# A two-layer hybrid encoder on one core: the start of layer 1 in written order up to the keys' product

## The chip, the core and the metric

One core of a Trainium2 chip runs the whole kernel: TensorE (PE) multiplies, VectorE (DVE), ScalarE (ACT) and GpSimd (POOL) work on tiles, SyncE (SP) issues most loads. The metric is the device time of one execution in microseconds (us), as the median of several runs. Before the change it is 1549.28 us, the median of 3 runs from 1547.82 to 1549.66.

## The reference, cut to what matters

Two layers are applied to 512 tokens of width 1024, all in float32. Each layer has a mixer (a Mamba-2 state-space part in both directions and windowed attention with 16 heads and 4 key-value heads) and a gated FFN. The piece that this case is about is the first stage of a layer:

```python
h = rms_norm(x, norm1_w[i])
proj = h @ w_in[i]
z, xbc, dt_raw, q, k, v = jnp.split(proj, [...], axis=-1)
xbc = jax.nn.silu(depthwise_conv_centered(xbc, conv_w[i], conv_b[i]))
dt = jax.nn.softplus(dt_raw + dt_bias[i])
a = -jnp.exp(a_log[i])
y_fwd = ssd_chunked(xs, dt[:, :, 0], a[0], bm, cm)
```

`ssd_chunked` needs running sums of `dt * a` over the tokens of a chunk of 128.

## The kernel before, in words

**Tiles.** The 512 tokens are four tiles of 128. A product in float32 is made of three float32r matmuls (`mm3`, lines 278 to 280 before): high part by high part, high by low, low by high. So each weight unit (a `raw` tile of at most 128 x 1024, one or two loads on SP's queue) is split by ScalarE into a high part (`whi`, line 161) and by VectorE into the rest (`wlo`, line 162), and each activation likewise.

**Weight units.** `prep_raw` issues the loads and `prep_split` the splits, in the order of a list: three units "vdt" (values and dt columns, 3, 3 and 2 of the 8 slices of the contraction), two "k" (keys), two each of bc0, q0, xa0 and so on. Three `raw` buffers and three pairs of split buffers are used in turn, so k0's split takes the buffers of vdt unit 0, and k0's load the `raw` buffer that vdt unit 0's split has freed.

**The first stage of layer 1.** `first_norm(t)` squares a token tile (ScalarE), makes the inverse root (POOL), scales the tile (VectorE), transposes it on TensorE and splits it (`turn_split`, lines 314 to 318) into `hT`. `vdt(t, j)` multiplies token tile t by unit j: 9, 9 or 6 matmuls of 288 columns. `bias_table` makes the table of the attention's bias. After the 96 matmuls of vdt, `setup` transposes the convolution's parameters with 42 small transposes (line 271), `dt_step` is softplus (one activation on ScalarE and 18 small operations on VectorE, lines 546 to 558), `dt_sums` makes the running sums by six matmuls with triangles of ones (line 574), `dt_own` takes logarithms (lines 593 to 601), and the keys, bc0, q0 and xa0 are each 48 matmuls of 512 columns, 24 by each of their two units (`ws_part`). `k_done` copies the keys out (lines 620 and 622).

**What sets the order.** In layer 1 the instructions up to the end of vdt stand under `tc.manual_schedule()`: each engine takes them in the order of the code. From there on (`start.close()`) a scheduler orders them by priority. Every engine works through its queue in order. A load on a hardware queue waits for the one issued eight loads before it.

Of the kernel before, what the change touches and what calls it, by code (L numbers as in the profile page):

```python
# [7 lines left out]
F32 = mybir.dt.float32  # L8
# [6 lines left out]
P = 128  # L15
L = 512
NT = L // P
D = 1024
# [21 lines left out]
WBUF = 3  # L40
RBUF = 3
# [5 lines left out]
def encoder_kernel(  # L47
# [23 lines left out]
    nc = tc.nc  # L71
# [21 lines left out]
    def nm(s):  # L93
        uid[0] += 1
        return f"{s}_{uid[0]}"
# [12 lines left out]
    splits = {}  # L108
# [26 lines left out]
    def prep_raw(n):  # L135
        while pos["raw"] < min(n, len(units)):
            key, (w, pieces) = units[pos["raw"]]
            raw = rawp.tile([P, 1024], F32, tag="raw", name=nm("raw"))
            for kt0, nkt, c0, ncol, off, pitch in pieces:
                dst = raw[:, : nkt * pitch].rearrange("p (k c) -> p k c", k=nkt)  # L140
                nc.sync.dma_start(dst[:, :, off : off + ncol], kcols(w, kt0, nkt, c0, ncol))
            raws[key] = raw
            pos["raw"] += 1
# [93 lines left out]
    wrow = npool0.tile([1, D], F32, name="wrow")  # L237
    nc.scalar.dma_start(wrow, norm1_w[0:1])
    nc.sync.dma_start(x_sb[0], x_in[0:P])
    prep_raw(1)  # L240
    nc.sync.dma_start(x_sb[1], x_in[P : 2 * P])
    prep_raw(2)
    nc.sync.dma_start(x_sb[2], x_in[2 * P : 3 * P])
    prep_raw(3)
    nc.sync.dma_start(x_sb[3], x_in[3 * P : 4 * P])

    ones = cp.tile([P, P], F32, name="ones")
    G.memset(ones, 1.0)
# [40 lines left out]
        G.tensor_tensor(rs, ms, mhalf.broadcast_to([P, width]), ALU.pow)  # L289
        return rs  # L290

    def first_norm(t):

        xn = npool0.tile([P, D], F32, tag="xn", name=nm("xn"), bufs=2)
        ss = smp.tile([P, 1], F32, tag="ss1", name=nm("ss"))
        S.activation(xn, x_sb[t], AF.Square, scale=1.0 / 32.0, accum_out=ss)
        rs = smp.tile([P, 1], F32, tag="rs1", name=nm("rs"))
        G.tensor_scalar(rs, ss, EPS, None, ALU.add)
        G.tensor_tensor(rs, rs, mhalf, ALU.pow)
        yield  # L300
        for b in range(2):
            cs = slice(512 * b, 512 * b + 512)
            V.scalar_tensor_tensor(xn[:, cs], x_sb[t][:, cs], rs, wb0[:, cs], ALU.mult, ALU.mult)
        yield
        for b in range(2):
            turn_split(xn, t, b, hT)
        yield

    def turn_split(xn, t, b, dst):
        ps = small_bank()  # L310
        pv = ps.rearrange("p (k c) -> p k c", k=4)
        for j in range(4):
            kt = 4 * b + j
            turn128(pv[:, j, :], xn[:, kt * P : (kt + 1) * P], ident)
        h, l = dst[b]
        hs, ls = h[:, :, t * P : (t + 1) * P], l[:, :, t * P : (t + 1) * P]
        S.copy(hs, pv)
        V.tensor_tensor(ls, pv, f(hs), ALU.subtract)
# [105 lines left out]

    def bcast(name, src, width):
        t = cp.tile([P, width], F32, name=name)
        nc.scalar.dma_start(t, src.unsqueeze(0).broadcast_to([P, width]))
        return t

    dtb_all = bcast("dtb_all", dt_bias.rearrange("a b c -> (a b c)"), DEPTH * 32)  # L430
# [39 lines left out]
    for i in range(DEPTH):  # L470
        side = Side()
        with ExitStack() as mix:
            ep = mix.enter_context(pool(f"mixer_{i}", bufs=1, reuse_waits="tile"))

            def g_ws(key, acts, done):

                banks = [dense_bank() for _ in range(2)]
                for j in range(2):
                    ws_part(key, j, acts, banks)
                    if j == 1:  # L480
                        done(banks)
                    yield
# [11 lines left out]
            def vdt(t, j):  # L494
                k0, n = ((0, 3), (3, 3), (6, 2))[j]
                hv, lv = (w[:, : n * 288].rearrange("p (k c) -> p k c", k=n) for w in vw[j])
                sl = slice(t * P, (t + 1) * P)
                for k in range(n):
                    kt = k0 + k
                    ah, al = hT[kt // 4]  # L500
                    mm3(vb[t][:, :288], ah[:, kt % 4, sl], al[:, kt % 4, sl], hv[:, k], lv[:, k], kt == 0, kt == KT - 1)
                if j == 2:
                    S.copy(v_sb[:, t, :], vb[t][:, :256])
                    V.tensor_tensor(xdt[:, t, :], vb[t][:, 256:288], dtb_all[:, 32 * i : 32 * i + 32], ALU.add)

            if i == 0:
                norms = [first_norm(t) for t in range(NT)]
                next(norms[0])
                next(norms[0])
                prep_split(1)  # L510
                next(norms[0])
                next(norms[1])
                next(norms[1])
                prep_split(2)
                next(norms[1])
                next(norms[2])
                next(norms[2])
                prep_split(3)
                vw = [splits.pop((i, "vdt", j)) for j in range(3)]
                vdt(0, 0)  # L520
                vdt(1, 0)
                vdt(0, 1)
                next(norms[2])
                next(norms[3])
                next(norms[3])
                vdt(1, 1)
                vdt(0, 2)
                vdt(1, 2)
                prep_raw(WBUF + RBUF)
                bias_table()  # L530
                next(norms[3])
                for t in (2, 3):
                    for j in range(3):
                        vdt(t, j)
                S.activation(expa_all, alog_all, AF.Exp)
                start.close()
            else:
                vw = [take((i, "vdt", j)) for j in range(3)]
                for t, j in ((t, j) for t in range(NT) for j in range(3)):
                    vdt(t, j)  # L540
# [3 lines left out]
            def dt_step():  # L544

                V.scalar_tensor_tensor(sp_e, xdt, -1.0, xdt, ALU.mult, ALU.min)
                S.activation(sp_e, sp_e, AF.Exp)
                V.tensor_scalar(sp_w, sp_e, 2.0, None, ALU.add)
                V.reciprocal(sp_w, sp_w)
                V.tensor_tensor(sp_w, sp_w, sp_e, ALU.mult)  # L550
                V.tensor_tensor(sp_w2, sp_w, sp_w, ALU.mult)
                V.tensor_scalar(sp_a, sp_w2, 1.0 / 17.0, None, ALU.mult)
                for n in (15, 13, 11, 9, 7, 5, 3):
                    V.scalar_tensor_tensor(sp_a, sp_a, 1.0 / n, sp_w2, ALU.add, ALU.mult)
                V.scalar_tensor_tensor(sp_a, sp_a, 1.0, sp_w, ALU.add, ALU.mult)
# [47 lines left out]
            if i == 0:  # L603
                setup()
                setupx.close()
                first.close()
            dt_step()


            mixA = []  # L610
# [10 lines left out]
                    for o in (0, HD):  # L621
                        V.tensor_tensor(kst_l[o : o + HD, h], src, f(kst_h[r : r + HD, h]), ALU.subtract)

            side.run(g_ws((i, "k"), hT, k_done), 0)

            class Item:
                pass
# [526 lines left out]
```

## Time and profile before

| | us |
|---|---|
| median of 3 runs | 1549.28 |
| lowest and highest run | 1547.82, 1549.66 |
| the profiled execution's own time | 1550.88 |
| its span | 1549.2 |
| mean granted clock of TensorE | 0.992 of full |

The profiled execution took 1.60 us more than the median, and 1.68 of its time lie around the span. In the rows below, times run from the span's start. A row of a timeline has the start and length in us, engine, line, operation, output<-inputs, partitions x elements, and in brackets the rest before it and what ended it. A row of a stretch has from:to, its length, the busy time of each engine with its instructions, and at the end the granted TensorE clock as a share of 2.4 GHz, the DMA engines' busy share and GB/s. PEld is the load of weights into TensorE, SPq an issue on SP's queue.

### The profile page before, as it was taken

The numbers are of one execution on the slowest core, as the hardware profiler recorded it, in microseconds if no ns is written. First come the engines' busy times: TensorE is split into PE (matmuls) and PEld (weight loads), VectorE is DVE, ScalarE is ACT, GpSimd is POOL, SyncE is SP. The second block draws the span as 40 slices with busy tenths as digits, with TensorE's granted clock in tenths as the row PEclk, the third lists the DMA queues.
The fourth block names the chain that finished last, engine by engine and source line by source line (L and its number), as shares of the span: only waits on it lengthen the run. The fifth ranks groups of instructions, "written<-read, shape, count | busy, mean of one in ns | idle before, by whom it ended". The sixth has DMA issues, their size and how long they took to land.

```text
span 1549.2 us, 20198 instructions
## 1 busy us (share of the span) xinstructions
PE 1512.3 (98%) x7680; PEld 1241.2 (80%) x7680; DVE 873.1 (56%) x1406; ACT 795.0 (51%) x1464; POOL 176.6 (11%) x246
## 2 busy tenths in 40 slices
PE   7999999999999999999999999999999999999997
PEld 6787778877888888888888777888778888888886
DVE  5677777676644444433367777777666434443333
ACT  4468988873443233323256788788535323332223
POOL 3000002424200000000020000053232000000002
PEclk9899999999999999999999999999999999999999
DMA  6522333453233333333343322345422333333321
GB/s 203 157 82 77 84 85 96 129 181 95 92 100 96 96 99 101 98 98 96 99 148 90 88 77 63 83 123 177 136 96 82 95 97 100 102 96 96 95 95 68
DMA packets 113079, 161.48 MB, mean 104 GB/s; under 512 B 7931, under 2 KB 90107, under 8 KB 112974
## 3 DMA queue, kind: packets, MB, share of 16 engines
q1 hardware_dynamic: 104756, 132.60, 28.0%
q0 software_dynamic: 7648, 27.50, 6.5%
q8 instruction: 60, 0.98, 0.3%
q14 instruction: 37, 0.30, 0.1%
q10 hardware_dynamic: 578, 0.10, 0.0%
HBM read 155.82 MB, written 8.55 MB: 106 GB/s over the span
## 4 chain that ended last, share of the span: by engine, by line
PE 88%; DVE 4%; issue 2%; ACT 2%; POOL 1%; DMA 1%; POOLq 0%; SPq 0%; DVEq 0%; ACTq 0%
PE pd L280 22%; PE pd L278 22%; PE pd L279 22%; PE psm L280 3%; PE psm L278 3%; PE psm L279 3%; PE psm L686 2%; PE psm L676 2%; PE psm L918 1%; PE psm L642 1%; PE psm L933 1%; PE psm L643 1%; PE psm L876 1%; DVE wlo L162 1%; ACT whi L161 1%
## 5 line engine op out<-in xcount | busy, mean ns | idle before, releaser
L278 PE MATMUL pd<-t,whi 128*128 128x512 f32 (+1 forms) x1088 | 420.0, 387 | 1.5 <-ACT whi L161 1.5
L279 PE MATMUL pd<-t,whi 128*128 128x512 f32 (+1 forms) x1088 | 419.4, 386 | 0.0
L280 PE MATMUL pd<-t,wlo 128*128 128x512 f32 (+1 forms) x1088 | 418.7, 385 | 0.4 <-DVE wlo L162 0.4
L162 DVE TENSOR_TENSOR wlo<-raw,whi 128x1024 fp32r<-128x1024 f32 (+1 forms) x214 | 260.5, 1221 | 239.7 <-ACT whi L161 239.0
L161 ACT CAST whi<-raw 128x1024 fp32r<-128x1024 f32 (+1 forms) x214 | 222.1, 1042 | 235.8 <-PE pd L279 207.3
L278 PEld LDWEIGHTS pd<-t,whi 128*128 128x128 f32 x1088 | 205.0, 189 | 40.2 <-ACT whi L161 1.7
L280 PEld LDWEIGHTS pd<-t,wlo 128*128 128x128 f32 x1088 | 204.9, 188 | 39.9 <-DVE wlo L162 1.2
L279 PEld LDWEIGHTS pd<-t,whi 128*128 128x128 f32 x1088 | 205.2, 189 | 37.8 <-issue 0.8
L278 PE MATMUL pd<-whi,t 128*128 128x256 f32 (+2 forms) x544 | 191.2, 351 | 0.0
L279 PE MATMUL pd<-wlo,t 128*128 128x256 f32 (+2 forms) x544 | 181.6, 334 | 4.0 <-DVE wlo L162 3.9
L280 PE MATMUL pd<-whi,t 128*128 128x256 f32 (+2 forms) x544 | 182.2, 335 | 0.6 <-DVE t L958 0.6
L279 PEld LDWEIGHTS pd<-wlo,t 128*128 128x128 f32 x544 | 105.4, 194 | 17.0 <-DVE wlo L162 4.6
L278 PEld LDWEIGHTS pd<-whi,t 128*128 128x128 f32 x544 | 105.3, 194 | 14.5 <-issue 4.6
L280 PEld LDWEIGHTS pd<-whi,t 128*128 128x128 f32 x544 | 105.2, 193 | 11.0 <-DVE t L958 1.5
L1096 ACT CAST ph<-t 128x512 fp32r<-128x512 f32 x40 | 25.0, 624 | 142.9 <-PE psm L279 132.5
L1097 DVE TENSOR_TENSOR pl<-t,ph 128x512 fp32r<-128x512 f32 x40 | 27.7, 692 | 114.8 <-ACT ph L1096 114.8
L395 DVE SCALAR_TENSOR_TENSOR sg<-pd,fprm,sg 128x511 f32<-128x511 f32 x88 | 65.9, 748 | 30.7 <-ACT sg L389 29.0
L644 DVE CUSTOM_DVE_ANT_0 s<-psm,bias,sink_all 128x256 f32<-128x256 f32 (+1 forms) x128 | 66.8, 547 | 24.6 <-POOL s L638 11.3
L658 ACT ACTIVATE s<-s,nm 128x257 f32<-128x257 f32 (+1 forms) x128 | 70.6, 556 | 3.4 <-DVE nm L655 3.2
L395 DVE SCALAR_TENSOR_TENSOR xT<-pd,cprm,xT 128x509 f32<-128x509 f32 (+2 forms) x96 | 67.5, 743 | 3.3 <-ACT xT L389 3.2
L278 PE MATMUL pd<-whi,ph 128*128 128x512 f32 x176 | 68.9, 391 | 0.0
L279 PE MATMUL pd<-wlo,ph 128*128 128x512 f32 x176 | 68.7, 390 | 0.0
(206 smaller groups left out, 2183.2 us busy)
## 6 DMA issues: line engine op xcount, KB each, us to landing
raw<-in_w_up_dram SPq DMA_DIRECT2D x88, 512.0 KB
raw<-in_w_in_dram SPq DMA_DIRECT2D x52, 512.0 KB
raw<-in_w_down_dram SPq DMA_DIRECT2D x44, 512.0 KB
rows<-sums POOLq DMA_DIRECT2D x32, 512.0 KB, 5.7
raw<-in_w_out_dram SPq DMA_DIRECT2D x32, 512.0 KB
bias<-toep POOLq DMA_DIRECT2D x16, 384.0 KB, 3.9
raw<-in_w_in_dram SPq DMA_DIRECT2D x18, 256.0 KB
x<-in_x_dram SPq DMA_DIRECT2D x8, 512.0 KB
```

The costliest lines, as they stand in the source:

```text
L161: S.copy(hi[:, :used], raw[:, :used])
L162: V.tensor_tensor(lo[:, :used], raw[:, :used], f(hi[:, :used]), ALU.subtract)
L278: mm(o, lh, rh, start=start, stop=False)
L279: mm(o, lh, rl, start=False, stop=False)
L280: mm(o, ll, rh, start=False, stop=stop)
L395: V.scalar_tensor_tensor(dst[:, lo:hi], src[:, lo + d : hi + d], taps[k], dst[:, lo:hi], ALU.mult, ALU.add)
L644: V.tensor_tensor_reduce(out=s4[:, h, :w], in0=ps[:, :w], in1=it.bias[h // 2][:, h % 2, it.j0 : it.j1], scale=1.0, scalar=sink4[:, h : h + 1],
L658: S.activation(s4[:, h, : w + 1], s4[:, h, : w + 1], AF.Exp, bias=nm4[:, h : h + 1], accum_out=den[:, h : h + 1])
L676: turn128(ps[:, c : c + P], it.s4[:, h, b * P : (b + 1) * P], ident)
L686: mm(po[c * HD : (c + 1) * HD, :256], v_sb[:, it.k0 // P + b, it.g * HD : (it.g + 1) * HD], it.pts[b][:, c * 256 : (c + 1) * 256], start=( ...
L1096: S.copy(h, p_sb[kt])
L1097: V.tensor_tensor(l, p_sb[kt], f(h), ALU.subtract)
```

## The change

It writes out the order of layer 1's first stage up to and including the keys' product.

- **Loads.** Tokens 0 and 1 are loaded first, then vdt unit 0, token 2, unit 1, token 3, unit 2. The four broadcast loads (dt bias, a_log, skip, sink) go to SP's queue, behind unit 2, instead of ScalarE's.
- **First norms.** The generator `first_norm` becomes `first_square`, `first_scale`, `first_turn`; tile t+1 is squared ahead of tile t's turn, with three buffers `xn` instead of two.
- **Products.** vdt(0,0) stands between the turns of tiles 0 and 1; the others are interleaved anew, by unit for tiles 2 and 3.
- **Keys.** The two keys' units are split as soon as vdt units 0 and 1 are used up, and the manual order goes on through `setup`, the keys' product and `dt_step`; the rest, `dt_sums` included, is left to the scheduler.

```diff
-    prep_raw(1)
-    nc.sync.dma_start(x_sb[1], x_in[P : 2 * P])
...
+    for t in range(1, NT):
+        nc.sync.dma_start(x_sb[t], x_in[t * P : (t + 1) * P])
+        prep_raw(t)
...
-        nc.scalar.dma_start(t, src.unsqueeze(0).broadcast_to([P, width]))
+        nc.sync.dma_start(t, src.unsqueeze(0).broadcast_to([P, width]))
...
             if i == 0:
-                norms = [first_norm(t) for t in range(NT)]
...
+                first_square(0)
+                first_scale(0)
+                first_square(1)
                 prep_split(1)
+                first_turn(0)
+                first_scale(1)
+                vw = [splits.pop((i, "vdt", 0))]
+                vdt(0, 0)
+                first_square(2)
                 prep_split(2)
+                first_turn(1)
+                vw.append(splits.pop((i, "vdt", 1)))
+                vdt(0, 1)
+                vdt(1, 0)
+                vdt(1, 1)
+                first_scale(2)
+                first_square(3)
                 prep_split(3)
+                prep_raw(WBUF + RBUF)
+                vw.append(splits.pop((i, "vdt", 2)))
+                first_turn(2)
+                first_scale(3)
                 vdt(0, 2)
                 vdt(1, 2)
                 bias_table()
+                vdt(2, 0)
+                first_turn(3)
+                vdt(3, 0)
+                prep_split(4)
+                vdt(2, 1)
+                vdt(3, 1)
+                prep_split(5)
+                vdt(2, 2)
+                vdt(3, 2)
                 S.activation(expa_all, alog_all, AF.Exp)
-                start.close()
...
-            dt_step()
+            else:
+                dt_step()
...
-            side.run(g_ws((i, "k"), hT, k_done), 0)
+            keys = g_ws((i, "k"), hT, k_done)
+            if i == 0:
+                next(keys)
+                dt_step()
+                for _ in keys:
+                    pass
+                start.close()
+            else:
+                side.run(keys, 0)
```

**On TensorE, behind vdt, before.** frow and nrow are the last parameter transposes, psm_732 takes the running sums, pd_483 and pd_484 the keys.

```order
L271 MATMUL psm_424<-ident,frow 128x8 x22
L271 MATMUL psm_448<-ident,nrow 128x2 x8
L574 MATMUL psm_732<-sp_406,t_le 128x64
L574 MATMUL psm_732<-sp_406,t_gt 128x64
L574 MATMUL psm_732<-sp_406,t_ge 128x64
L574 MATMUL psm_732<-sp_406,t_lt 128x64
L574 MATMUL psm_732<-sp_406,ones 128x64 x2
L278 MATMUL pd_483<-t_10_121,whi_485 128x512
L279 MATMUL pd_483<-t_11_122,whi_485 128x512
```

The keys' first products stand behind the running sums. The same place now:

```order
L268 MATMUL psm_431<-ident,frow 128x8 x22
L268 MATMUL psm_455<-ident,nrow 128x2 x8
L275 MATMUL pd_472<-t_10_121,whi_370 128x512
L276 MATMUL pd_472<-t_11_122,whi_370 128x512
L277 MATMUL pd_472<-t_10_121,wlo_371 128x512
```

The keys follow the parameter transposes at once. And behind q0 (pd_653 is its second bank, pd_744 the first bank of xa0):

```order
L277 MATMUL pd_653<-t_12_123,wlo_605 128x512
L581 MATMUL psm_732<-sp_413,t_le 128x64
L581 MATMUL psm_732<-sp_413,t_gt 128x64
L581 MATMUL psm_732<-sp_413,t_ge 128x64
L581 MATMUL psm_732<-sp_413,t_lt 128x64
L581 MATMUL psm_732<-sp_413,ones 128x64 x2
L275 MATMUL pd_744<-t_10_121,whi_654 128x512
```

The running sums have moved behind the 144 matmuls of the keys, bc0 and q0.

**On ScalarE, before, from the last copy of the values (v) to the keys' splits.** whi_485 and whi_489 are k0 and k1, whi_493 and whi_526 bc0, the rows named sp are softplus and dt_own, ex is the running sums' exponential.

```order
L503 COPY v_177<-pd_187 128x256
L535 ACTIVATE expa_all<-alog_all 128x64
L547 ACTIVATE sp_406<-sp_406 128x128
L594 ACT_TABLE_LOAD
L594 ACTIVATE sp_409<-sp_407 128x128
L595 ACT_TABLE_LOAD
L595 ACTIVATE sp_408<-sp_409 128x128
L575 ACTIVATE ex_180<-psm_732 128x384
L161 CAST whi_485<-raw_326 128x1024
L577 COPY run_182<-psm_732 128x4x16 x2
L161 CAST whi_489<-raw_328 128x1024
```

Both keys' splits stand behind five activations and two table loads. The same place now, with whi_370 and whi_392 for k0 and k1, whi_474 and whi_525 for bc0 (t_12 is the last token tile's split):

```order
L319 CAST t_12_123<-psm_354 128x4x128
L161 CAST whi_370<-raw_294 128x1024
L161 CAST whi_392<-raw_296 128x1024
L505 COPY v_177<-pd_186 128x256
L505 COPY v_177<-pd_187 128x256
L543 ACTIVATE expa_all<-alog_all 128x64
L161 CAST whi_474<-raw_298 128x1024
L554 ACTIVATE sp_413<-sp_413 128x128
L161 CAST whi_525<-raw_478 128x1024
```

The keys' splits stand in front of the last copies of the values and of softplus; dt_own's two table loads stand further down.

**On SP, the first loads before.** x_1 to x_4 are the token tiles, raw_94, raw_98 and raw_102 the vdt units (two loads each), crow the first of nine parameter loads.

```order
L239 DMA x_1_87<-in_x_dram 128x1024
L141 DMA raw_94<-in_w_in_dram 128x3x256
L141 DMA raw_94<-in_w_in_dram 128x3x32
L241 DMA x_2_88<-in_x_dram 128x1024
L141 DMA raw_98<-in_w_in_dram 128x3x256
L141 DMA raw_98<-in_w_in_dram 128x3x32
L243 DMA x_3_89<-in_x_dram 128x1024
L141 DMA raw_102<-in_w_in_dram 128x2x256
L141 DMA raw_102<-in_w_in_dram 128x2x32
L245 DMA x_4_90<-in_x_dram 128x1024
L457 DMA crow<-in_conv_w_dram 7x1536
```

Tokens and units alternate from the first on. Now, with raw_95, raw_99 and raw_103 for the units:

```order
L239 DMA x_1_87<-in_x_dram 128x1024
L241 DMA x_2_88<-in_x_dram 128x1024
L141 DMA raw_95<-in_w_in_dram 128x3x256
L141 DMA raw_95<-in_w_in_dram 128x3x32
L241 DMA x_3_89<-in_x_dram 128x1024
L141 DMA raw_99<-in_w_in_dram 128x3x256
L141 DMA raw_99<-in_w_in_dram 128x3x32
L241 DMA x_4_90<-in_x_dram 128x1024
L141 DMA raw_103<-in_w_in_dram 128x2x256
L141 DMA raw_103<-in_w_in_dram 128x2x32
L429 DMA dtb_all<-in_dt_bias_dram 128x64
L429 DMA alog_all<-in_a_log_dram 128x64
```

Tile 1 stands in front of unit 0, and the four broadcasts (two more follow) in front of the parameters. Behind the first attention blocks of layer 1 every engine has the order it had before.

## Rows read from the trace of the kernel before

**Rows 1.** The page: busy time of the engines, us, share of the span, instructions.
```profile
PE 1512.3 (98%) x7680; PEld 1241.2 (80%) x7680; DVE 873.1 (56%) x1406; ACT 795.0 (51%) x1464; POOL 176.6 (11%) x246
```

**Rows 2.** Stretches, from:to and length, then busy time and instructions of each engine.
```profile
15.05:35.57 20.52, 20.52 (x158) 19.11 (x156) 9.66 (x21) 8.22 (x18) 5.16 (x9) 1.00 0.51 161
35.57:40.46 4.89, 0.01 (x1) 0.03 (x1) 4.44 (x15) 0.62 (x1) 2.02 (x5) 0.57 1.02 323
40.46:44.77 4.31, 2.80 (x13) 2.61 (x13) 1.30 (x7) 3.38 (x7) 0.00 (x0) 0.50 1.00 289
44.77:50.69 5.92, 5.92 (x15) 4.68 (x16) 3.81 (x5) 2.06 (x4) 0.00 (x0) 0.57 0.79 246
```

**Rows 3.** Timeline of TensorE: start, length, line, tiles, count, rest before it.
```profile
34.94 0.63 PE L271 MATMUL psm<-ident,nrow 2*128 2x2 f32 x8
40.46 0.66 PE L574 MATMUL psm<-sp,t_le 128*128 128x64 f32 x2 [4.89 <-DVE sp L593]
...
79.96 0.39 PE L278 MATMUL pd<-t,whi 128*128 128x512 f32 x1
```

**Rows 4.** Waits from 33 to 50 us: in total, times, longest.
```profile
PE psm L574 <- DVE sp L593: 4.9, 1, 4.9
```

**Rows 5.** Timelines of VectorE and ScalarE: softplus begins, k0's split.
```profile
34.26 0.29 DVE L546 SCALAR_TENSOR_TENSOR sp<-xdt 128x128 f32<-128x128 f32 x1
...
44.74 1.23 DVE L162 TENSOR_TENSOR wlo<-raw,whi 128x1024 fp32r<-128x1024 f32 x1 [0.57 <-ACT whi L161]
...
43.68 1.04 ACT L161 CAST whi<-raw 128x1024 fp32r<-128x1024 f32 x1
```

**Rows 6.** Layer 2: running sums and next product on TensorE, and a stretch.
```profile
835.41 0.33 PE L574 MATMUL psm<-sp,t_le 128*128 128x64 f32 x2
...
836.66 0.48 PE L278 MATMUL pd<-t,whi 128*128 128x512 f32 x1
...
800.00:850.00 50.00, 49.53 (x240) 41.45 (x239) 37.91 (x72) 30.95 (x48) 0.00 (x0) 1.00 0.38 106
```

**Rows 7.** The start: timelines of TensorE, ScalarE and VectorE.
```profile
13.43 1.97 PE L314 MATMUL psm<-ident,xn 128*128 128x128 f32 x8 [3.83 <-DVE xn L303]
...
18.80 0.44 PE L278 MATMUL pd<-whi,t 128*128 128x288 f32 x1
19.04 0.37 PE L279 MATMUL pd<-wlo,t 128*128 128x288 f32 x1
...
19.51 0.29 PE L279 MATMUL pd<-wlo,t 128*128 128x288 f32 x1
19.64 0.29 PE L280 MATMUL pd<-whi,t 128*128 128x288 f32 x1
...
25.29 1.23 PE L314 MATMUL psm<-ident,xn 128*128 128x128 f32 x8
...
4.43 1.06 ACT L296 ACTIVATE xn<-x 128x1024 f32<-128x1024 f32 x1 [1.58 <-DMA x<-in_x_dram]
...
8.68 0.91 ACT L161 CAST whi<-raw 128x864 fp32r<-128x864 f32 x1 [3.10 <-DMA raw<-in_w_in_dram]
...
26.60 0.69 DVE L318 TENSOR_TENSOR t<-psm,t 128x512 fp32r<-128x512 f32 x1 [0.34 <-ACT t L317]
```

**Rows 8.** Two stretches of rest; the granted clock is the third number from the end.
```profile
36.25:36.50 0.25, 0.00 (x0) 0.00 (x0) 0.21 (x1) 0.00 (x0) 0.25 (x1) 0.51 1.05 311
287.05:288.75 1.70, 0.00 (x0) 0.00 (x0) 1.43 (x2) 1.68 (x2) 0.23 (x1) 1.00 0.00 0
```

**Rows 9.** Timeline of SP's queue: loads issued.
```profile
0.80 0.39 SPq L239 DMA_DIRECT2D x<-in_x_dram  x1
...
2.24 0.49 SPq L241 DMA_DIRECT2D x<-in_x_dram  x1
...
10.84 0.37 SPq L457 DMA_DIRECT2D crow<-in_conv_w_dram  x1
...
16.96 38.48 SPq L141 DMA_DIRECT2D raw<-in_w_in_dram  x9
```

More of the change, by code (lines that the diff above doesn't have):

```diff
@@ L239, in encoder_kernel @@
     nc.sync.dma_start(x_sb[0], x_in[0:P])
-    prep_raw(1)
-    nc.sync.dma_start(x_sb[1], x_in[P : 2 * P])
[L242 to L245, printed above, removed]
+    for t in range(1, NT):
+        nc.sync.dma_start(x_sb[t], x_in[t * P : (t + 1) * P])
+        prep_raw(t)
     ones = cp.tile([P, P], F32, name="ones")
@@ L290, in rstd_of, with first_square @@
         return rs
-    def first_norm(t):
-        xn = npool0.tile([P, D], F32, tag="xn", name=nm("xn"), bufs=2)
+    first_xn = {}
+    def first_square(t):
+        xn = npool0.tile([P, D], F32, tag="xn", name=nm("xn"), bufs=3)
         ss = smp.tile([P, 1], F32, tag="ss1", name=nm("ss"))
@@ L299, in first_norm, with first_scale @@
         G.tensor_tensor(rs, rs, mhalf, ALU.pow)
-        yield
+        first_xn[t] = xn, rs
+    def first_scale(t):
+        xn, rs = first_xn[t]
         for b in range(2):
@@ L303, in first_norm, with first_turn @@
             V.scalar_tensor_tensor(xn[:, cs], x_sb[t][:, cs], rs, wb0[:, cs], ALU.mult, ALU.mult)
-        yield
+    def first_turn(t):
         for b in range(2):
-            turn_split(xn, t, b, hT)
-        yield
+            turn_split(first_xn[t][0], t, b, hT)
     def turn_split(xn, t, b, dst):
@@ L506, in encoder_kernel @@
             if i == 0:
-                norms = [first_norm(t) for t in range(NT)]
-                next(norms[0])
-                next(norms[0])
+                first_square(0)
+                first_scale(0)
+                first_square(1)
                 prep_split(1)
-                next(norms[0])
-                next(norms[1])
-                next(norms[1])
-                prep_split(2)
-                next(norms[1])
-                next(norms[2])
-                next(norms[2])
-                prep_split(3)
[L519 to L526, printed above, removed]
+                first_turn(0)
[3 more added lines that the diff above has]
+                first_square(2)
+                prep_split(2)
+                first_turn(1)
[5 more added lines that the diff above has]
+                first_square(3)
+                prep_split(3)
+                prep_raw(WBUF + RBUF)
+                vw.append(splits.pop((i, "vdt", 2)))
+                first_turn(2)
+                first_scale(3)
                 vdt(0, 2)
                 vdt(1, 2)
-                prep_raw(WBUF + RBUF)
                 bias_table()
[L531 to L534, printed above, removed]
+                vdt(2, 0)
[7 more added lines that the diff above has]
+                vdt(3, 2)
                 S.activation(expa_all, alog_all, AF.Exp)
-                start.close()
             else:
```

## The prediction

> **What bounds the kernel now.** I read the page's busy times first. TensorE is busy 1512.3 us of a span of 1549.2 [rows 1], so only its 36.9 us of rest, and stretches at its lower clock, can be won. The cut into stretches then shows where they lie in the part that the change touches [rows 2]: TensorE works without a pause from 15.05 to 35.57 us, rests 4.9 us to 40.46, then does 2.80 us of work in 4.31 us, and from 44.77 to 50.69 is busy at a mean granted clock of 0.57, that is mostly at 1.2 of 2.4 GHz. The timeline of TensorE names the work [rows 3]: at 34.94 the last parameter transposes, at 40.46 the running sums (`dt_sums`), from 44.77 the products of the keys, bc0 and q0, 144 in all, and at 79.96 the first product of xa0. The waits and the timelines say why [rows 4, 5]: `dt_sums` waited 4.9 us for VectorE, whose softplus ran from 34.26 to past 40 us. The keys stood behind `dt_sums` on TensorE; on ScalarE the keys' first split stood behind the activations of `dt_step`, `dt_own` and `dt_sums` and began at 43.68. Both keys' units had been asked for at 16.96 [rows 9] and their buffers were there; nothing but the order held them.
>
> **The change, part by part.**
>
> *Keys in front of the sums.* After the change the parameter transposes are followed on TensorE by the keys, and `dt_sums` comes after q0. The rest from the end of the transposes (34.94 + 0.63 = 35.57) to 44.77 goes: **9.2 us**. This needs k0's split in time. Its buffer is vdt unit 0's and comes free with the product vdt(3,0), which is followed by 30 products of 0.13 us and 2.75 us of transposes, 6.7 us in all; ScalarE's copy (1.04 us) and VectorE's difference (1.23 us) take 2.3 [rows 5]. k1 comes 18 products (2.4 us) after k0, and the keys' first half takes 24 products of 0.227 us, 5.4 us. So both splits are hidden, with over 4 us to spare.
>
> *The clock.* At rest the granted clock fell to 0.50 within 36.25 to 36.50 us [rows 8], and the first 15 products, 44.77 to 50.69, took 5.92 us [rows 2]. The other 129, 50.69 to 79.96 [rows 3], took 0.227 us each, so 15 would take 3.4. If the clock stays up, **2.5 us** go.
>
> *The sums, put back.* In layer 2 of this same kernel `dt_sums` already stands behind q0: 835.41 to 836.66, **1.25 us** on the path [rows 6]. Softplus, 6.2 us of VectorE, and `dt_own` then run beside 144 products (32.7 us). Layer 2 shows that this cover holds: TensorE is busy 49.53 of 50 us there [rows 6].
>
> *The start.* Three edits, taken together. (1) vdt(0,0), 9 products, moves in front of token tile 1's turn. TensorE rested there before: tile 1's turn starts at 13.43 after 3.83 us of rest [rows 7]. vdt(0,0) needs the first unit's split, which began at 8.68 [rows 7] and takes two engines about 1 us each, and tile 0's split behind it; at the lower clock's pitch of 0.24 us (18.80 to 19.04, [rows 7]) it lasts 2.2 us and fits into the gap. So 2.2 us less work stands behind the turn. (2) vdt(3,0) now follows tile 3's turn at once. That turn ended at 26.52 and the first half of the split behind it (0.69 us from 26.60) at 27.29 [rows 7]: some 0.7 us is a new wait of TensorE. (3) Squaring a tile ahead puts 1.2 us of ScalarE (1.06 and the read of its sum, [rows 7]) in front of the first unit's copy, which had waited 3.10 us for its load, so it costs nothing while that wait lasts. Sum: **+1.5 us**.
>
> Bounds for the start. Above: with more products early the clock may be up by 15.4 us, the end of tile 1's turn, instead of 19.04 (from there the pitch is 0.13, 19.51 to 19.64, [rows 7]); 15 products times 0.11 us give 1.7 more, 3.2. Below: tile 1 is now loaded in front of the first weight unit. Tile 0, issued at 0.80 [rows 9], was there at 4.43 [rows 7], so a tile takes at most 3.6 us; if the unit came later by all of that, the start would lose 2.1. I stay at 1.5: tile 1's load was already asked for at 2.24 [rows 9], ahead of the unit's landing, and so shared its time before.
>
> *Queues.* SP now issues four broadcast loads that ScalarE issued before, ahead of the nine parameter rows and of k0. The nine held it from 10.84 to 16.96 [rows 9], 0.68 us each; four more make 2.7 us, k0 at 19.7 instead of 16.96, for a split that starts near 27. ScalarE gains the issue time while it waits for tile 0 anyway. POOL's order is unchanged. Nothing here reaches the path. After the first attention blocks of layer 1 all engines have the orders they had before, so what is won early stays.
>
> **Sum**: 9.2 + 2.5 - 1.25 + 1.5 = 11.95 us. The profiled execution took 1550.88 (span 1549.2); less 11.95 it would be 1538.9. The median of the runs is 1.6 lower, 1549.28, and gives **1537.3 us**.
>
> **The rivals.**
>
> *The clock falls at the parameter transposes.* The 42 transposes have 16 columns or fewer each. Before, the granted clock was down at 36.25 to 36.50, under 1 us after the last of them, while a rest of 1.7 us behind full products, 287.05 to 288.75, left it at 1.00 [rows 8]. If the transposes weigh as rest, the clock may fall on the keys although TensorE never stops: then the 2.5 us stay, 9.45 are won, 1539.8 us. Against it: in what the rows show 4.9 us of rest followed them, and now the keys do. The Trainium skill, page "TensorE: Matmul & The Clock Gate", section "Part 4: PE-mode transpose", has the rule that the full clock "doesn't engage for transpose-mode"; by it this rival would be the likelier one, 1539.8, and the rows on the fall agree in direction. I give it 0.27.
>
> *The moved VectorE work comes onto the path.* Softplus and `dt_own` now share the stretch in which VectorE evacuates the keys and begins bc0's convolution. If all 6.2 us of softplus delayed a bank that TensorE waits for, 5.75 are won: 1543.5. Against it: layer 2 does all this in the same order and rests 0.47 us in 50 [rows 6]. 0.05.
>
> *Slower than before: k0's load comes too late.* The place is SP's queue: each issue waits for an earlier load to land, and k0 stands behind 13 small loads. To lose all of the 11.95 us, the keys would have to start at 34.1 + 11.95 = 46, so k0 would have to land at 43.7 and, a load taking at most 3.6, be asked for at 40.1. From 10.84 on that is 2.25 us for each of the 13, where the nine cost 0.68 [rows 9]. Were they to cost 2.5, the keys would start near 49.2 and the time be 1552.5. Against it: the price would have to be over three times as high. 0.02.
>
> *Nothing comes of it.* TensorE would rest elsewhere for as long, at a load that ends at a fixed hour. I find none: the attention's bias is asked for long before its first use. 0.03.
>
> **How the numbers follow.** The forecast has 0.63, the clock rival 0.27, the VectorE rival 0.05, no change 0.03, slower 0.02. From the first two with the start's bounds: best 11.95 + 1.7 = 13.65, 1535.6; worst 11.95 - 2.5 - 3.6 = 5.85, 1543.4, but both ends at once are unlikely, and I cut at 1542. Below I add the 1.5 us by which a run lies under the median (1547.82 against 1549.28): 1534 to 1542. A measurement of this kernel can tell about 0.2%, 3.1 us, from no change; every case of the first three wins more. So faster 0.95, within 0.2% 0.03, slower 0.02.
>
> **What would show it.** Right: in the changed profile the keys' first product follows the last parameter transpose within 0.3 us, near 34 us; no wait of `dt_sums` on VectorE; the first product of xa0 near 68 us instead of 79.96, with the granted clock at 1.00 from 34 us on. The clock rival: products of 0.43 us at the keys' start. The start: parameter transposes beginning near 31.3 instead of 32.82, and a wait of some 0.7 us behind tile 3's turn. Wrong: TensorE resting for k0's split or for a bank of q0, or a first xa0 product later than 73 us.

## The result and the profile after

The changed kernel takes **1538.92 us** (median of 4 runs, 1537.70 to 1539.58) against 1548.55 (1546.66 to 1549.66) for the kernel before on the same chip: a ratio of 0.9944, 95% interval 0.9931 to 0.9956, faster by 9.6 us. Another five runs of the same kernel, below, gave 0.9950 (0.9937 to 0.9962). Forecast were 1537.3, a gain of 11.95 us, and a range of 1534 to 1542. The two profiled executions lie further apart, 1549.2 against 1536.0 of span, 13.2 us; the other 3.6 are taken up with the second profile of the kernel before.

The page of the changed kernel, busy times. TensorE is busy for 4.8 us less than in [rows 1], and rests 28.5 us instead of 36.9:

```profile
PE 1507.5 (98%) x7680; PEld 1235.0 (80%) x7680; DVE 873.1 (57%) x1406; ACT 794.6 (52%) x1464; POOL 176.5 (11%) x246
```

TensorE's timeline, answering to [rows 3, 7]. Line numbers are three lower than before in `mm3` and `setup`:

```profile
29.31 0.91 PE L268 MATMUL psm<-ident,crow 16*128 16x16 f32 x12
...
31.44 0.63 PE L268 MATMUL psm<-ident,nrow 2*128 2x2 f32 x8
32.00 0.50 PE L275 MATMUL pd<-t,whi 128*128 128x512 f32 x1
...
66.57 0.33 PE L581 MATMUL psm<-sp,t_le 128*128 128x64 f32 x2
...
67.83 0.48 PE L275 MATMUL pd<-t,whi 128*128 128x512 f32 x1
...
75.60 0.36 PE L659 MATMUL psm<-t,q 128*128 128x256 f32 x1 [1.36 <-DVE q L732]
```

The keys follow the transposes of the parameters at once, at 32.00 instead of 44.77. `dt_sums` runs at 66.57 without a wait and costs 1.26 us, and xa0 begins at 67.83 instead of 79.96: 12.13 us ahead. The last row is new: the attention's scores wait 1.36 us for q.

Stretches of the changed kernel, as in [rows 2] (the granted clock is the third number from the end):

```profile
29.31:32.00 2.69, 2.69 (x44) 2.67 (x43) 1.66 (x5) 1.46 (x3) 0.08 (x1) 1.00 1.04 354
32.00:33.28 1.28, 1.28 (x7) 1.04 (x6) 1.17 (x2) 0.00 (x0) 1.28 (x2) 0.98 0.80 236
33.28:36.67 3.39, 3.39 (x9) 2.67 (x8) 2.81 (x9) 0.31 (x1) 0.66 (x4) 0.51 0.81 265
36.67:66.57 29.90, 29.90 (x132) 24.51 (x131) 20.61 (x35) 15.23 (x21) 0.00 (x0) 1.00 0.60 187
```

TensorE never stops here, and the clock falls all the same: the granted clock is 0.51, that is 1.2 of 2.4 GHz, from 33.28 to 36.67. The first 15 products of the keys took 5.12 us, where 5.92 stood before and 3.4 was forecast.

The start of the changed kernel, ScalarE's and TensorE's timelines:

```profile
8.00 0.91 ACT L161 CAST whi<-raw 128x864 fp32r<-128x864 f32 x1 [1.26 <-DMA raw<-in_w_in_dram]
...
12.53 1.14 PE L316 MATMUL psm<-ident,xn 128*128 128x128 f32 x8
...
14.07 0.29 PE L277 MATMUL pd<-whi,t 128*128 128x288 f32 x1
...
23.50 0.40 PE L275 MATMUL pd<-whi,t 128*128 128x288 f32 x1 [0.24 <-ACT t L319]
```

Tile 1's turn begins at 12.53, behind vdt(0,0) and without a rest (13.43 after 3.83 us of rest in [rows 7]), and products go at 0.13 us from 14.07 on (19.25 before). The granted clock reads 1.00 on both sides of that change of pitch (9.96 to 14.07, and 14.07 to 17.00), as it does in the first stretch of [rows 2]: what the prediction calls the lower clock at the start is read from the products' pitch alone. The transposes of the parameters begin 3.5 us sooner. Behind tile 3's turn TensorE waits 0.24 us, and 0.19 once more.

### The profile page after: what moved, and what is told of

The parts are those of the page before. It is cut to its first block, busy times and chain, and to the rows that moved or that the text cites. A ratio compares the mean times of both kernels' runs of the same rounds, so it can differ in the third digit from the quotient of the medians.

```text
span 1536.0 us, 20195 instructions
## 1 busy us (share of the span) xinstructions
PE 1507.5 (98%) x7680; PEld 1235.0 (80%) x7680; DVE 873.1 (57%) x1406; ACT 794.6 (52%) x1464; POOL 176.5 (11%) x246
## 4 chain that ended last, share of the span: by engine, by line
PE 81%; DVE 6%; ACT 4%; issue 4%; DMA 3%; POOL 2%; POOLq 0%; DVEq 0%; ACTq 0%; SPq 0%
PE pd L277 20%; PE pd L276 20%; PE pd L275 20%; PE psm L277 3%; PE psm L275 3%; PE psm L276 3%; PE psm L703 2%; PE psm L693 2%; DVE wlo L162 2%; PE psm L935 1%; PE psm L659 1%; PE psm L950 1%; DMA raw<-in_w_in_dram 1%; ACT whi L161 1%; DMA bias<-toep 1%
## 5 line engine op out<-in xcount | busy, mean ns | idle before, releaser
L275 PEld LDWEIGHTS pd<-whi,t 128*128 128x128 f32 x544 | 103.5, 190 | 16.3 <-issue 4.8
L277 PEld LDWEIGHTS pd<-whi,t 128*128 128x128 f32 x544 | 103.4, 190 | 11.6 <-DVE t L975 1.4
L275 PE MATMUL pd<-whi,ph 128*128 128x512 f32 x176 | 68.9, 391 | 0.0
```

Source lines behind the costliest of these rows:

```text
L275: mm(o, lh, rh, start=start, stop=False)
L277: mm(o, ll, rh, start=False, stop=stop)
```

## A second profile of both kernels, and the marks of all runs

Two runs repeat the kernels unaltered, to see what in a profile belongs to the kernel.

**e12, the kernel before again.** Expected:

> The kernel before unaltered, for a second profile. Theory (the first profile's span, 1549.2 us, had two falls of the clock near 288 and 1046 us that cost 3.4 us, and a median run has fewer): the first product of xa0 within 0.8 us of 79.96, and the span below 1549.2 by 1.7 or 3.4 us if one or both falls are missing, unchanged if both are there. Rival (the two profiles differ in the early part, so that the 13.2 us between the profiles are not those of the median runs): xa0 more than 1 us earlier than 79.96.

**e11, the changed kernel again.** Expected:

> The changed kernel unaltered, for a second profile and for its time on the chip of these runs. Theory (what differs between profiles of one kernel are stretches at the lower clock, near 33 us, 285 us and 1040 us, of some 1.7 us each, and nothing else): the marks up to the first product of xa0 agree with those of the first profile within 0.5 us unless the clock fell otherwise, and the span differs by what the falls explain within 0.7 us. Rival (the work itself comes at other times from run to run): the marks differ by more at the full clock.

Measured: e12 one run of 1547.06 us, span 1545.3; e11 1540.65 us (1539.08 to 1541.60), ratio 0.9950 (0.9937 to 0.9962), span 1537.4. All marks that the text uses stand in one table, read from TensorE's timeline of each run (us). "15 keys" is the time from the first to the sixteenth product of the keys; "bank" is a wait of TensorE for VectorE's evacuation of the keys (`k_done`), "q" that of the scores for q; the last column is the ratio to the kernel before on the same chip, with its interval.

| run | parameters | keys | 15 keys | xa0 | scores | bank | q | ratio |
|---|---|---|---|---|---|---|---|---|
| before | 32.82 | 44.77 | 5.92 | 79.96 | 85.40 | 0 | 0 | 1 |
| before, e12 | 31.75 | 43.70 | 5.35 | 78.30 | 83.74 | 0 | 0 | one run |
| changed | 29.31 | 32.00 | 5.12 | 67.83 | 73.36 | 0 | 1.36 | 0.9944 (0.9931-0.9956) |
| changed, e11 | 28.67 | 31.36 | 5.14 | 67.28 | 72.81 | 0 | 1.33 | 0.9950 (0.9937-0.9962) |
| e1 keys only | 32.12 | 34.81 | 5.14 | 72.55 | 78.09 | 1.84 | 1.36 | 0.9976 (0.9966-0.9985) |
| e2 start only | 29.34 | 40.67 | 5.08 | 74.99 | 80.43 | 0 | 0 | 0.9984 (0.9975-0.9994) |
| e7 split behind | 30.68 | 35.18 | 12.44 | 76.87 | 82.31 | 0 | 0 | 0.9981 (0.9972-0.9990) |
| e6 turn first | 31.27 | 33.96 | 3.53 | 70.24 | 75.77 | 2.00 | 1.36 | 0.9973 (0.9963-0.9982) |
| e5 old loads | 31.46 | 34.14 | 3.53 | 71.07 | 76.61 | 2.64 | 1.37 | 0.9964 (0.9952-0.9976) |
| e3 spread | 26.80 | 33.14 | 3.53 | 68.03 | 73.57 | 0.60 | 1.35 | 0.9950 (0.9937-0.9963) |
| e4 sums later | 29.07 | 31.75 | 5.14 | 67.51 | 73.13 | 1.07 | 1.71 | 0.9941 (0.9929-0.9954) |
| e9 both | 26.75 | 33.09 | 3.53 | 66.94 | 72.64 | 0.83 | 1.67 | 0.9942 (0.9930-0.9954) |
| e10 bias later | 27.71 | 32.46 | 5.58 | 68.54 | 74.08 | 0 | 0.25 | 0.9944 (0.9931-0.9958) |
| e13 copy later | 28.72 | 31.41 | 5.13 | 67.03 | 72.57 | 0 | 0.25 | 0.9939 (0.9925-0.9953) |

Two things follow. First, the early marks of one kernel differ by up to 1.7 us between its profiles: in e12 the products of vdt reached the 0.13 us pitch at 16.86 instead of 19.25, and the clock came back behind the keys' start at 47.65 instead of 49.99. My rival for e12 was right here: the profile that the prediction was built on was one of the longer ones. The marks of e11 lie 0.55 to 0.64 us ahead of the first profile's, a little outside the 0.5 of its theory. And e7, below, has the changed kernel's start, yet reached that pitch at 16.37 instead of 14.07. Second, late falls of the clock come and go, each at the same place. All 14 profiles have a rest of TensorE near 280 us, in 12 of them 1.95 us long, and one of 1.95 us near 1040. The first of these rests and the work behind it, in the first profile of before and in e12:

```profile
287.05:288.99 1.94, 0.00 (x0) 0.00 (x0) 1.67 (x3) 1.92 (x2) 0.23 (x1) 0.96 0.00 0
288.99:292.15 3.16, 3.16 (x14) 3.16 (x15) 1.74 (x3) 3.13 (x7) 0.00 (x0) 0.50 0.62 170
```

```profile
285.38:287.33 1.95, 0.00 (x1) 0.00 (x0) 1.67 (x3) 1.93 (x2) 0.24 (x1) 1.00 0.00 0
287.33:291.00 3.67, 3.67 (x30) 3.67 (x31) 2.25 (x3) 3.64 (x9) 0.18 (x1) 1.00 0.60 196
```

Of the 14 profiles 8 show such a fall between 276 and 294 us and 11 one between 1035 and 1050; the first profile of before has both, that of the changed kernel neither. The lead of the changed kernel over the first profile of before steps up by 1.4 us at the first place and by 0.9 at the second. So of the 13.2 us between those two profiles about 2.3 are such falls. The early stretch gave 12.0 us at the first scores, 10.5 behind the wait for q and 9.6 at 250 us; the remaining 1.2 come between the two falls, 0.8 of them between 320 and 400 us, and what brings them stays open. Against e12 the lead at the scores is 83.74 - 73.36 = 10.4. With the 1.4 for q taken off, that is 9.0 us, and 8.1 are left at 250 us; the medians have 9.6 and 7.5. The change's worth is about 8 to 10 us, not 13.

## The experiments

**e1, the keys alone, and e2, the start alone.** e1 takes the kernel before and makes only the later edit, shown here; e2 takes the changed kernel and undoes the same lines:

```diff
+                        if t == 3 and j < 2:
+                            prep_split(4 + j)
...
-                start.close()
...
-            dt_step()
+            else:
+                dt_step()
...
-            side.run(g_ws((i, "k"), hT, k_done), 0)
+            keys = g_ws((i, "k"), hT, k_done)
+            if i == 0:
+                next(keys)
+                dt_step()
+                for _ in keys:
+                    pass
+                start.close()
+            else:
+                side.run(keys, 0)
```

> Only the later part of the change: the splits of the keys' first two weight units ahead, and the keys in front of softplus and dt_sums; the start (loads, squares, order of the turns) as in the kernel before. Theory (the parts add up, and each pays in its own stretch): the setup transposes begin near 32.8 us as before, the keys' first product follows them at about 35.6 instead of 44.77, the first product of xa0 comes at 71 to 71.5 instead of 79.96 (9.2 won, up to 0.8 more by the clock, 1.25 given back for dt_sums), and the time falls by 7.5 to 9 us. Rival (the keys' gain needs the earlier start, because with the old loads the first unit's split is late): the keys start at 38 us or later and less than 6 us is won.

> Only the first part of the change: the loads paired anew, squares a tile ahead, tile 0's vdt in front of tile 1's turn; the splits of the keys' weight, softplus and dt_sums stay where they were before. Theory: the setup transposes begin near 29.3 us instead of 32.82, TensorE then rests for softplus as before, the keys start near 41.2, xa0 near 76.5, and the time falls by 3 to 4 us. Rival (the stretch ahead of the keys is bound by something that does not move with the start, the keys' load or the chain to softplus): the setup is earlier, and the rest behind it grows by the same; xa0 at 79 or later, and no more than 1 us is won.

e1 had the keys at 34.81, as the theory had it: from the first parameter transpose to the keys it took 2.69 us, where both profiles of the kernel before have 11.95. But xa0 came at 72.55, not 71 to 71.5, because of a wait that neither side had named. TensorE's and ScalarE's timelines of e1:

```profile
63.04 0.47 PE L278 MATMUL pd<-t,whi 128*128 128x512 f32 x1 [1.84 <-DVE t L624]
...
49.40 1.05 ACT L161 CAST whi<-raw 128x1024 fp32r<-128x1024 f32 x1 [12.61 <-DMA raw<-in_w_in_dram]
```

ScalarE stood 12.6 us before the load of one weight unit, VectorE's evacuation of the keys came late behind it, and TensorE waited for the bank. The time fell by 3.1 us, not 7.5 to 9. e2 did what its theory said in the trace: parameters at 29.34, keys at 40.67, and no wait for q; xa0 came 1.5 us ahead of its 76.5. In time it won 2.7 us (0.6 to 2.5 per thousand by its ratio), just under 3 to 4. Against the first profile of before the leads at the scores add up, 7.3 and 5.0 where both together have 12.0; against e12 they do not, 5.7 and 3.3 where both have 10.4. The medians add to 5.8, where both together won 7.5 to 9.6. By the intervals, some 1.5 us either way for each, that difference is not shown to be one.

**e7, the order in front of the keys undone.**

```diff
-                prep_split(4)
-                prep_split(5)
...
-                next(keys)
```

> The changed kernel without the early splits of the keys' first two units and with softplus and dt_sums in front of the keys, its start and everything else kept, so that TensorE rests for softplus again. Theory: the setup begins at 29.3, the keys' first product comes at 40 to 41.5 instead of 32.00, xa0 at 75.5 to 77 instead of 67.83, and the time is 8 to 9 us above the changed kernel's. Rival (the order in front of the keys alone is worth little, what matters is when the keys' weight is there, and the rest is made good behind the keys): keys before 37 us, and less than 5 us lost.

TensorE made two products of the keys at 35.18, behind a wait of 1.74 us for their split, and then rested for softplus as before:

```profile
35.18 0.79 PE L275 MATMUL pd<-t,whi 128*128 128x512 f32 x1 [1.74 <-ACT whi L161]
...
39.89 0.66 PE L579 MATMUL psm<-sp,t_le 128*128 128x64 f32 x2 [3.50 <-DVE sp L563]
```

xa0 came at 76.87, 9.0 us behind the changed kernel's, inside the theory's 75.5 to 77. Of these 9.0, 1.4 were lost ahead of the edit's place, since the parameters began at 30.68 and not at 29.31; 7.7 belong to the order in front of the keys. Neither side had foreseen the two products at 35.18; the third came at 42.44, later than the theory's 40 to 41.5. In time 5.8 us were lost, not 8 to 9 (1544.71 against 1538.92, on another chip; by the ratios 0.9981 and 0.9944): this kernel has no wait for q, so it is spared the 1.4 that the changed one pays. The keys' order is the larger part of the gain.

**e6 and e5, what brought the start.** e6 puts tile 1's turn back in front of vdt(0,0); e5 puts the loads back (each weight unit ahead of the next token, the broadcasts on ScalarE's queue):

```diff
 # e6
-                vdt(0, 0)          # behind first_scale(1)
+                vdt(0, 0)          # behind first_turn(1)
 # e5
-        nc.sync.dma_start(x_sb[t], x_in[t * P : (t + 1) * P])
         prep_raw(t)
+        nc.sync.dma_start(x_sb[t], x_in[t * P : (t + 1) * P])
```

> The changed kernel, with tile 1's turn put back in front of tile 0's vdt. Theory (the start won 3.5 us instead of 1.5 because tile 0's products fill TensorE's wait for tile 1's norm, and the granted clock then rises some 6 us sooner): the products of vdt go at the slow pitch until past 18 us again, the setup transposes begin 2 to 3.5 us later than 29.3, that is at 31.5 to 32.8, xa0 at 70 to 71.3 instead of 67.83, and the time is 2 to 3.5 us above the changed kernel's. Rival (the loads and the squares brought the start): the setup begins before 30.3, and the time is within 1 us of the changed kernel's.

> The changed kernel, with the old pairing of the loads: each weight unit asked for ahead of the next token tile, and the first layer's broadcast rows asked for by ScalarE's queue again. Theory (the start was won by the order on TensorE and the loads carry little): the setup begins at 29.3 to 29.8 us, and the time is within 0.5 us of the changed kernel's. Rival (the pairing of the loads brought the 0.7 us by which the first weight's split and tile 1's norm came earlier): tile 1's turn is later, the setup begins at 30 to 31.5, and the time is 0.7 to 2 us above.

Each of the two costs 2 us of the start when undone: parameters at 31.27 (e6) and 31.46 (e5). My theory for e5 fell; its rival had the start right (30 to 31.5). Its ScalarE and TensorE show why the loads matter:

```profile
9.17 1.06 ACT L295 ACTIVATE xn<-x 128x1024 f32<-128x1024 f32 x1 [2.85 <-DMA x<-in_x_dram]
...
10.22 0.90 ACT L161 CAST whi<-raw 128x864 fp32r<-128x864 f32 x1
...
11.65 0.61 PE L275 MATMUL pd<-whi,t 128*128 128x288 f32 x1 [1.54 <-ACT t L319]
```

With tile 1 squared ahead, its square stands on ScalarE in front of the first unit's copy; with the old loads it waits 2.85 us for its tile, and the copy comes at 10.22 instead of 8.00. The edits need each other. In e6 vdt's products reached the fast pitch at 15.37, not past 18 as I had written; its 2.0 us go with the rest of 2.49 us before tile 1's turn, which vdt(0,0) no longer fills. Both also paid a wait for the bank, 2.00 and 2.64 us, and both won 1.6 at the keys: at the scores they stand 2.4 and 3.3 us behind the changed kernel. In time e6 was 4.5 us above it by the ratios and e5 3.1; what e6 lost beyond its 2.4 is within what these intervals leave open.

e5 and e6 hold another finding. In both the block of transposes runs exactly as in the changed kernel, and the clock does not fall. Stretches of e6, the block and the keys' first 15 products:

```profile
31.27:33.96 2.69, 2.69 (x43) 2.67 (x43) 1.66 (x5) 1.46 (x3) 0.12 (x1) 1.00 1.03 367
33.96:37.49 3.53, 3.53 (x17) 2.92 (x16) 2.98 (x6) 0.31 (x1) 1.85 (x5) 1.00 0.83 257
```

**e3, the transposes spread.** `some(5)` issues the next five of the 42:

```diff
+                if i == 0 and (t, j) in ((2, 1), (3, 1), (2, 2), (3, 2)):
+                    some(5)        # behind the products of vdt(t, j)
```

> The changed kernel, with the 42 transposes of the parameters spread in portions of five matrices among the products of vdt for tiles 2 and 3, none left as a block in front of the keys. Theory (the block of transposes, 2.7 us in which TensorE issues transposes alone, is what the clock falls on: 0.43 us a product from 33.28 to 36.27): the clock stays at 1.00 through the keys, their first 15 products take 3.4 us instead of 5.12, xa0 comes at 66 to 66.5 instead of 67.83, and the time falls by 1.3 to 1.8 us against the changed kernel's. Rival (the clock falls there for another reason, the waits of 0.2 us or the mere time since it rose): the slow products are still there at about the same place, and the time is within 0.5 us of the changed kernel's.

The edit does less than its text says: 15 of the 42 left the block, and 27 still ran as one in front of the keys, 1.8 us long. The clock stayed at 1.00 and the 15 products took 3.53 us instead of 5.12, as the theory had it. The time did not follow (ratio 0.9950, where the changed kernel has 0.9944 and 0.9950): the keys began at 33.14, 1.1 us later (1.8 later than in e11), and TensorE then waited 0.60 us for the bank. xa0 came at 68.03, not at 66 to 66.5. Since a block is left here, and e5 and e6 keep the clock with the whole of it, e3 does not show that the block is what makes the clock fall. Two other profiles come nearer to it. In e12, the kernel before, the clock fell at 33.92, with TensorE still in the block, without a rest and without the keys; the block up to its last eight transposes, and these eight (the granted clock is the third number from the end):

```profile
31.75:33.87 2.12, 2.12 (x35) 2.12 (x35) 0.90 (x5) 0.87 (x4) 0.00 (x0) 1.00 1.05 386
33.87:34.83 0.96, 0.96 (x11) 0.87 (x9) 0.93 (x2) 0.96 (x1) 0.01 (x1) 0.53 0.98 350
```

In e10 it fell at 30.04, with the last transpose at 30.45. In the changed kernel, e1, e4, e11 and e13 it fell 0 to 1.2 us behind the block, with TensorE busy.

**e4, the sums later, and e9, both.**

```diff
-            later = {1: dt_sums, 3: dt_rows, 5: dt_own}
+            later = {1 + (i == 0): dt_sums, 3: dt_rows, 5: dt_own}
```

> The changed kernel, with dt_sums of layer 1 taken up one dense group later. Theory (the exponential of dt_sums with the load of its table stands on ScalarE in front of the fourth copy of q, and the scores wait 1.36 us for it): the wait of the scores on q at 75.6 us is gone or below 0.3 us, and 1 to 1.4 us is won. Rival (the wait only moves, to the next thing that the exponential stands in front of): a wait of about the same size shows up within the next 20 us, and the time is within 0.5 us of the changed kernel's.

> The changed kernel with both edits, the transposes of the parameters spread among vdt and dt_sums one dense group later. Theory (both are worth what they save, in different stretches): 15 key products in 3.4 us and no wait of the scores for q; 2.3 to 3.2 us below the changed kernel's, so about 1536. Rival (neither is on the path, or one eats the other): within 1 us of the changed kernel's.

The theory fell; as far as the intervals tell, the times are the changed kernel's, as both rivals had it. Without the exponential in the way the scores still waited for q, 0.86 and 0.85 us, and TensorE 1.07 for the bank. e9 gave 0.9942, the changed kernel's time. So something earlier than `dt_sums` made q late.

**e10 and e13, the load behind it.** The changed kernel's timelines from POOL, SP, ScalarE and VectorE:

```profile
25.14 2.99 POOL L261 DMA_DIRECT2D toep<-table  x4 [2.49 <-DMA table<-tb]
...
27.78 9.37 SPq L141 DMA_DIRECT2D raw<-in_w_in_dram  x4
...
45.29 1.05 ACT L161 CAST whi<-raw 128x1024 fp32r<-128x1024 f32 x1 [11.31 <-DMA raw<-in_w_in_dram]
...
46.38 1.23 DVE L162 TENSOR_TENSOR wlo<-raw,whi 128x1024 fp32r<-128x1024 f32 x1 [6.83 <-ACT whi L161]
```

and the stretch in which this load (bc0's second unit) is under way:

```profile
28.00:45.00 17.00, 17.00 (x103) 14.46 (x102) 8.63 (x24) 2.93 (x6) 2.15 (x6) 0.90 0.97 331
```

It was asked for at 27.78 and split at 45.29. The DMA engines were 0.97 busy all that time, most of it with the bias table's loads that POOL had asked for from 25.14 on (from 28 to 46 us POOL's queue took 68.9% of their time, SP's 27.5%). ScalarE and VectorE, in order, stood behind the split, and the keys' evacuation, the convolution of bc0 and q ran late. In the kernels with the old order in front of the keys (before, e2, e7) ScalarE does not stand there, and no wait for q occurs. e10 takes the bias table up behind `setup`; e13 leaves its two matmuls and moves only VectorE's copy, on which the loads hang:

```diff
 # e10
-                bias_table()       # behind vdt(1, 2)
+                bias_table()       # behind setup()
 # e13
         mm(ps_tb[:32, :], rb, oh, start=True, stop=True)
+        yield                      # goes on behind prep_split(5)
         V.tensor_copy(tb[:, 127:384], ps_tb[:32, 127:384])
```

> The changed kernel, with the attention's bias table (two products of TensorE, a copy of VectorE and the loads that POOL issues behind it) taken up behind the parameter transposes instead of in front of tile 2's vdt, some 9 us later. Theory (the wait of the scores on q comes from a load: bc0's second unit, asked for at 27.8 us, shares the DMA engines with the loads of the bias table, lands only at 45.3, and holds ScalarE for 11.3 us and VectorE for 6.8; the evacuations, the convolution and the fourth copy of q then run late): ScalarE waits for that unit 4 us at most, VectorE's rest at 39.5 us shrinks to under 3 us, the wait of 1.36 us on q is below 0.4, and the time is 1 to 2.2 us below the changed kernel's of the same chip. Rival 1 (the exponential of dt_sums alone makes q late): ScalarE's wait goes, that on q stays above 1 us, and the time is within 0.6 us. Rival 2 (the loads of the bias now come too late): a new wait of the scores for the bias, and a longer time.

> The changed kernel, with the two products of the bias table where they are, and only VectorE's copy of their result, with the loads that hang on it, moved from behind tile 2's third vdt product to behind the second keys' split, some 8 us; TensorE's order stays. Theory: as in the run with the whole table moved, ScalarE's wait of 11.3 us for bc0's second unit goes, and so does the wait of 1.36 us on q; since TensorE does the same in the same order, the keys start at 31.3 to 32.5 us and the clock falls on them at most as in the changed kernel (15 products in 5.12 us or less), so the scores stand 1.0 to 1.5 us ahead of the changed kernel's and the time falls by as much. Rival (the stretch at the lower clock after the parameters follows from something else than TensorE's order, so that it can grow here too): the wait goes, but the first 15 products take over 5.8 us, and the time is within 0.6 us of the changed kernel's.

In both the wait for q is down to 0.25 us and the wait for the load is gone. ScalarE's timeline of e10 and of e13, and TensorE's wait for q in e13:

```profile
40.10 1.05 ACT L161 CAST whi<-raw 128x1024 fp32r<-128x1024 f32 x1 [5.45 <-PE pd L276]
...
38.60 1.05 ACT L161 CAST whi<-raw 128x1024 fp32r<-128x1024 f32 x1 [5.20 <-PE pd L276]
```

```profile
PE psm L662 <- DVE q L735: 0.2, 1, 0.2
```

The copy now waits only for its buffer, which TensorE frees; so it waits 5.45 us in e10, where the theory had 4 at most. e13 has the same keys as e11 (31.41 and 31.36, 5.13 and 5.14 us for 15 products), so the two can be laid beside each other: at the scores it leads by 0.24 us, and behind q by 1.31, from 75 us on to 180 (the same product of the attention begins at 124.13 in e11 and at 122.82 in e13). In the time, 1538.43 us (1536.92 to 1539.86), ratio 0.9939 (0.9925 to 0.9953); the changed kernel's two intervals overlap it, so that e13 beats it is shown in the trace and not in the times. In e10 the bias matmuls and the keys behind the block ran at the lower clock, 5.58 us for 15 products; xa0 came 1.26 us behind that of e11, which took back what the wait had given, and the time did not move. Rivals 1 and 2 both fell.

## Why the prediction was right, and which steps were not

The time lies in the forecast's range and the largest step held; two other steps were mis-sized and one cost was missing. The gain of the medians, 9.6 and 7.5 us, is smaller than the 11.95 forecast, and the clock rival's 1539.8 lies nearer to 1538.92 than the forecast's 1537.3.

- **Keys in front of the sums, 9.2 us: right.** The keys follow the transposes within 0.1 us in every kernel with this edit but e10, which puts two products between. From the first transpose to the keys it takes 2.69 us in the changed kernel, e11 and e1, against 11.95 in both profiles of before: 9.26.
- **The clock, 2.5 us: wrong.** "If the clock stays up" did not hold; the rival that gave it 0.27 came true. Only 0.8 us was won against the first profile, 0.2 against the second. Against the rival the prediction held that in its rows 4.9 us of rest followed the transposes; in e12, the same kernel, and in e10 the clock fell before the last transpose, so the rest was not needed. Why the same block kept the clock in e5 and e6 stays open. The other row that the prediction set beside this one was misread: the rest that "left it at 1.00" [rows 8] is cut at 288.75 there; it lasted to 288.99, and the clock fell at 288.85, within it. The Trainium skill, page "TensorE: Matmul & The Clock Gate", section "Part 4: PE-mode transpose", says that the full clock does not engage for transpose-mode. The trace agrees only in part: the changed kernel runs the whole block at a granted clock of 1.00, and the first 15 products behind it took 5.12 us there but 3.53 in e5 and e6.
- **The sums put back, 1.25 us: right,** 1.26.
- **The start, 1.5 us: too small,** 3.5 against the first profile and 2.4 against the second. The sum took vdt(0,0) in the gap (2.2) and missed that it also brings the faster pitch from 19.25 to 14.07, which stood in my upper bound of 3.2; the first profile's 3.5 lies outside even that. The wait behind tile 3's turn was 0.43 us in all, not 0.7. "Squaring a tile ahead costs nothing" is true only together with the new loads (e5).
- **"Queues ... nothing here reaches the path": wrong,** and the missing cost. k0 was asked for at 15.94, even sooner than before, so the slower rival had no ground. But I looked at k0 alone. The split of k0, moved up, frees the buffer for bc0's second unit, which is so asked for while the bias table's loads fill the DMA engines: 1.36 us at q in the changed kernel. This is the rival on VectorE's work by another road: its work came late because ScalarE stood before a load, not because there was too much of it.

The sum of the real terms at xa0 is 9.2 + 3.5 + 0.8 - 1.26 = 12.2, against 12.13 in the trace and 11.95 forecast: the errors of the start and of the clock cancelled, which was luck. That the total came out so near also hangs on the first profile of before: against e12 the terms are 9.2 + 2.4 + 0.2 - 1.26 = 10.5, and the trace has 78.30 - 67.83 = 10.47. Behind that, 1.4 goes at q and up to 0.9 in the attention. Where these 0.9 go no run shows.

## What to carry to other kernels

When an edit moves a split or any other release of a buffer earlier, follow the load that the freed buffer asks for, and look at who holds the DMA engines at that time: an engine that works in order stands behind it with all that it has to evacuate. Undo each part alone as well, since parts that "cost nothing" may do so only together. And take a second profile of the kernel before when a few microseconds matter: here one kernel's marks moved by 1.7 us, and falls of the clock worth 0.9 to 1.4 us came and went.

## What the runs showed of the chip that I had not expected

- A clock that stays up can be worth nothing. e3, e5, e6 and e9 won 1.6 us at the keys and waited 0.60 to 2.64 us for the bank instead, with bc0's second unit split at 45.5 to 48.5 us, no sooner than in the changed kernel (45.29). To join e3 with e13 would show whether both can be had; it was not tried.
- The same work did not fix the clock. Behind or within the block of transposes it fell in eight profiles in which TensorE did not rest there first (the changed kernel, e1, e4, e7, e10, e11, e12 and e13), and in e5 and e6 it did not. At the same rest of 1.95 us near 280 us it fell in 8 of 12 profiles, from 0.2 us before the end of the rest to 0.6 behind it. What decides stays open.
- A weight unit of 512 KB took 17.5 us from being asked for to its split in the changed kernel (27.78 to 45.29), with the DMA engines 0.97 busy from 28 to 45 us, and 18.7 in e4 (27.54 to 46.19).
